# Bias rows of the four gates on SP's queue, and the general expert path as a loop over single experts

## The chip, the core and the metric

The kernel runs on one core of a Trainium2 chip. The metric is the device time of one execution in microseconds. The core has five engines that each work through a queue of their own, strictly in order: TensorE (PE in the profile, with its weight loads as PEld), VectorE (DVE), ScalarE (ACT), GpSimd (POOL) and SyncE (SP), which computes nothing and only issues transfers here. Transfers (DMAs) can be issued from SP, ACT and POOL.

## What is computed

A decoder trunk of two layers on 256 tokens of width 1024, all in float32. Layer 0 mixes tokens with a state-space scan (S5), layer 1 with forgetting attention (FoX) over a shared K and V. After each mixer comes a mixture of experts: 32 experts in four groups, two experts per token. Every sub-layer has a shift, a scale and a gate that depend on a conditioning vector `c`:

```python
def adaln(c, w, b, n):
    mod = jax.nn.silu(c) @ w + b
    return jnp.split(mod, n, axis=-1)

for l in range(DEPTH):
    shift, scale, gate = adaln(c, ada_w[l, 0], ada_b[l, 0], 3)
    ...
    h = h + gate[:, None, :] * mix
    shift, scale, gate = adaln(c, ada_w[l, 1], ada_b[l, 1], 3)
    ...
    h = h + gate[:, None, :] * hier_moe(...)
```

The four gates (`gate`, twice per layer) are what one part of the change touches: `b` is the bias row. The other part touches the sum over the experts:

```python
for e in range(N_EXPERTS):
    y = (jax.nn.silu(t @ w1[e]) * (t @ w3[e])) @ w2[e]
    out = out + gates[:, e:e + 1] * y
```

## The kernel before

**Weights.** All large weights stream once through a ring of slots of 1 MB (`new_slot`, `fetch`, line 67), every transfer issued by SP. `block` takes the next block, `prefetch` asks for one ahead of its use. A transfer waits in SP's queue until its slot is free. In the built program the transfers of SP and ACT also share eight completion counters that they take in turn, so that a transfer waits until the one eight places before it has landed. Which instruction follows which on an engine is settled when the program is built: a planner walks through a simulated timeline and, apart from parts with an order written out by hand (`tc.manual_schedule`), puts what is ready earliest first.

**Gates.** `ada_gate_pe` (lines 175 to 195) makes one gate: GpSimd clears a tile `rows` (line 179, it waits until the tile's last user, often `as_columns` at lines 139 to 141, is done), ACT issues two transfers of 2 KB that put the two halves of the bias into partitions 0 and 32 (line 181), TensorE multiplies four weight blocks (line 184), VectorE adds product and `rows` (line 188), and two matmuls (line 194) and ScalarE (line 195) spread the result over the partitions. It runs four times: in the S5 part (`gb00`, from the list `side`), at the start of the first mixture (`gb01`), in the FoX part (`gb10`) and at the start of the second mixture (`gb11`).

**S5 part.** Before its loop (lines 987 to 1014) stand `drive_u(0)` to `drive_u(2)` (TensorE, line 808), `prepare_b(0)` (VectorE lines 843 to 853, then ScalarE line 855, which copies from the tile `braw`), `flip_b(0)` (TensorE line 864, ScalarE line 867), and `direct(0)` (line 897). In the loop, `drive` (TensorE line 916, VectorE line 921) and the scans (line 935) follow.

**Experts.** In `moe`, each expert has 32 places for tokens (`CAP`). `experts` works through eight sets of four experts: `first` (line 506) and `second` (line 521) are the matmuls with the blocks `wa` and `wb`, `gather` and `scatter` move the tokens. Ahead of the seventh set stands `overflow` (lines 533 to 592): where some expert has more than 32 tokens (`mosti`, read into every engine), a loop over all experts adds what didn't fit; otherwise every engine branches over it (line 535). The inputs of this case don't take it.

Of the kernel before, what the change touches and what calls it, by code (L numbers as in the profile page):

```python
# [10 lines left out]
F32 = mybir.dt.float32  # L11
# [3 lines left out]
AF = mybir.ActivationFunctionType  # L15
OP = mybir.AluOpType
# [6 lines left out]
NE = 32  # L23
CAP = 32
NQ = NE // 4
# [13 lines left out]
def trunk(ctx: ExitStack, tc: tile.TileContext, A, out, ring=12, ring2=4, ring3=5, ring4=3, ring5=4, lpb=2, TK=2):  # L39
    nc = tc.nc  # L40
    V, S, G, PE = nc.vector, nc.scalar, nc.gpsimd, nc.tensor
# [9 lines left out]
    def acc_tile():  # L51
        return psum.tile([128, 512], F32, tag="acc", name="acc", bufs=4)

    def mm_tile():
        return psum.tile([128, 512], F32, tag="mm", name="mm", bufs=4)
# [14 lines left out]
    def block(name, *idx):  # L70
        for i, (b, t) in enumerate(ahead):
            if b == (name, idx):
                del ahead[i]
                return t
        if (name, idx) in later:
            later.remove((name, idx))
        return fetch(A[name][idx])
# [24 lines left out]
    ident = const.tile([128, 128], F32, name="ident")  # L102
# [18 lines left out]
    def sc32(k):  # L121

        return sc[:, k:k + 1].to_broadcast([128, 32])
# [4 lines left out]
    for q in range(4):  # L128
        r = slice(32 * q, 32 * q + 32)
# [45 lines left out]
    def ada_gate_pe(name, j, li, gbc, at_once=False):  # L175

        ps = mm_tile() if at_once else acc_tile()
        rows = small.tile([128, 512], F32, tag="rows", name="rows", bufs=1)
        G.memset(rows, 0.0)
        for n in range(2):  # L180
            nc.scalar.dma_start(rows[32 * n:32 * n + 1, :], A["gbias"][li, n:n + 1, :])
        for b, w in enumerate([block(name, j, b) for b in range(4)]):
            for q in range(4):
                PE.matmul(ps[32 * q:32 * q + 32, :], sc32(2 * b + q // 2), w[:, 512 * q:512 * q + 512],
                          start=b == 0, stop=b == 3)
            if not at_once:
                yield
        ins = V.tensor_tensor(rows, ps, rows, op=OP.add)
        if not at_once:
            tc.keep_in_program_order(ins)  # L190
        yield
        for n in range(2):
            pt = mm_tile()
            PE.matmul(pt, pick[:, n:n + 1].to_broadcast([128, 128]), rows, start=True, stop=True)
            S.activation(gbc[:, 512 * n:512 * n + 512], pt, AF.Copy)
# [136 lines left out]
    def moe(l, sh, g, gbc, c36, slots_):  # L332
# [12 lines left out]
        mb = []  # L345
# [21 lines left out]
        def t2(n, w):  # L367
            return ma.tile([128, 2, w], F32, name=n)
# [78 lines left out]
        scs, xgs, Ps, acc = {}, {}, {}, []  # L447
# [43 lines left out]
        def turned(a):  # L491
            pa = mm_tile()
            for f in range(2):
                PE.transpose(pa[:, 128 * f:128 * f + 128], a[:, 128 * f:128 * f + 128], ident)
            aT = mb[0].tile([128, 256], F32, tag="aT", name="aT", bufs=2)
            V.tensor_copy(aT, pa[:, 0:256])
            return aT
# [35 lines left out]
        def overflow(rv):  # L533

            with tc.If(rv > CAP):
                gov = t2("gov", NE)
                V.tensor_scalar(gov, rk, float(CAP) + 0.5, None, op0=OP.is_gt)
                V.tensor_tensor(gov, gov, gates, op=OP.mult)
                hnT = [mb[0].tile([128, KD, 128], F32, tag="y", name="hnT", bufs=2) for _ in range(2)]
                for i in range(2):  # L540
                    x = mb[0].tile([128, 256], F32, tag="aT", name="dr", bufs=2)[:, 0:128]
                    V.tensor_scalar(x, ident, rstd[:, i:i + 1], None, op0=OP.mult)
                    for kk in range(2):
                        pt = mm_tile()
                        for k4 in range(4):
                            k = 4 * kk + k4
                            o = pt[:, 128 * k4:128 * k4 + 128]
                            PE.matmul(o, h[:, i, 128 * k:128 * k + 128], x, start=True, stop=True)
                            V.tensor_scalar(hnT[i][:, k, :], o, g[:, k:k + 1], sh[:, k:k + 1],
                                            op0=OP.mult, op1=OP.add)  # L550
                with tc.For_i(0, NQ, 1) as q:
                    gcol = t2("gcol", 4)
                    G.dma_start(gcol, gov.rearrange("p i (q s) -> p i q s", s=4)[:, :, bass.ds(q, 1), :]
                                      .rearrange("p i o s -> p i (o s)"))
                    for s in range(4):
                        c = slice(512 * s, 512 * s + 512)

                        def part(name, j):
                            w = mb[0].tile([128, 2, 512], F32, tag="ow", name="ow", bufs=1)
                            G.dma_start(w, A[name][l, bass.ds(q, 1), 2 * j:2 * j + 2, :, c]  # L560
                                              .rearrange("o k p n -> p (o k) n"))
                            return w

                        ph = [mm_tile() for _ in range(2)]
                        for kp in range(4):
                            w = part("wa", kp)
                            for i in range(2):
                                for kk in range(2):
                                    PE.matmul(ph[i], hnT[i][:, 2 * kp + kk, :], w[:, kk],
                                              start=kp + kk == 0, stop=kp == 3 and kk == 1)  # L570
                        aTs = []
                        for i in range(2):
                            a = mb[0].tile([128, 256], F32, tag="a", name="oa", bufs=2)
                            S.activation(a, ph[i][:, 0:256], AF.Silu)
                            V.scalar_tensor_tensor(a, a, gcol[:, i, s:s + 1], ph[i][:, 256:512],
                                                   op0=OP.mult, op1=OP.mult)
                            aTs.append(turned(a))
                        for n in range(2):
                            w = part("wb", n)
                            py = [mm_tile() for _ in range(2)]  # L580
                            for f in range(2):
                                for i in range(2):
                                    PE.matmul(py[i], aTs[i][:, 128 * f:128 * f + 128], w[:, f],
                                              start=f == 0, stop=f == 1)
                            for i in range(2):
                                for c2 in range(2):
                                    r = slice(256 * c2, 256 * c2 + 256)
                                    t = mb[0].tile([128, 256], F32, tag="aT", name="ot", bufs=2)
                                    V.tensor_tensor(t, py[i][:, r], gbc[:, 512 * n + 256 * c2:512 * n + 256 * c2 + 256],
                                                    op=OP.mult)  # L590
                                    PE.matmul(acc[i][n][:, r], ident, t, start=False, stop=False,
                                              skip_group_check=True)

        def start(gated, ssq, fill, after):

# [78 lines left out]
    hnT = sp.tile([128, KD, T], F32, name="hnT")  # L674
# [28 lines left out]
    p, two = exp_parts(sp, ldt, t32)  # L703
# [13 lines left out]
    for b in range(2):  # L717
        r = slice(16 * b, 16 * b + 16)
# [6 lines left out]
    p, two = exp_parts(sp, z, t32)  # L725
# [11 lines left out]
    for b in range(4):  # L737
        r = slice(8 * b, 8 * b + 8)
# [73 lines left out]
    for m in range(2):  # L812
# [3 lines left out]

    steps = [1, 1, 1, 0, 1, 0, 1, 0, 0, 0]
    side = [ada_gate_pe("ada00g", 0, 0, gb00, True),
            ada_cols_pe("ada01", 0, as_shift(C_ADAB + 16, sh01)),
            ada_cols_pe("ada01", 1, as_gain(C_ADAB + 16, C_LNG + 8, g01)),  # L820
            ada_cols_pe("kvada", 0, as_shift(C_ADAB + 64, shkv)),
            ada_cols_pe("kvada", 1, as_gain(C_ADAB + 64, C_KVG, gkv))]
    fill = [ada_gate_pe("ada01", 2, 1, gb01)]


# [205 lines left out]
    def split_w(w):  # L1031
        o = gp.tile([128, 2, 512], F32R, tag="ws", name="ws", bufs=3)
        S.activation(o[:, 0], w, AF.Copy)
        V.tensor_tensor(o[:, 1], w, o[:, 0].bitcast(F32), op=OP.subtract)
        return o
# [10 lines left out]
    for n in range(2):  # L1046
        pg = [mm_tile() for _ in range(2)]
        for m in range(8):
            if m % 4 == 0:
                w = block("woutg", n, m // 4)  # L1050
            o = split_w(w[:, 512 * (m % 4):512 * (m % 4) + 512])
            if n == 0 and m < 7:
                split_u(m + 1)
            for i in range(2):
                for u, b in ((uH, 0), (uL, 0), (uH, 1)):
                    PE.matmul(pg[i], u[:, m, 128 * i:128 * i + 128], o[:, b], start=m == 0 and b == 0 and u is uH,
                              stop=m == 7 and b == 1)
# [563 lines left out]
```

## Time and profile before

| | us |
|---|---|
| median of 3 runs (849.17 to 849.5) | 849.39 |
| the profiled execution | 854.14 |
| its span, first to last instruction | 852.5 |
| TensorE busy | 722.5 (85%) |
| VectorE busy | 410.1 (48%) |
| ScalarE busy | 218.3 (26%) |
| GpSimd busy | 58.3 (7%) |
| moved by DMA | 299.32 MB |

The profiled execution is slower than the timed ones, and 1.64 us of it lie outside its span. "busy" of TensorE holds pipelined matmuls and is not its share of peak. A wait is shown as the idle time of an engine, with what ended it; a wait for several things is put down to the one that came last. Queue instructions (issue, semaphore, branch) are marked with a q behind the engine (ACTq) and don't count as busy. The profile gives TensorE's clock as the share that was granted, 1.0 being 2.4 GHz and 0.5 being 1.2 GHz.

### The profile page before, as it was taken

What the parts mean: (1) busy time and instruction counts of PE and PEld (TensorE: products, weight loads), DVE (VectorE), ACT (ScalarE), POOL (GpSimd) and SP (SyncE); (2) the same over time, 40 slices, a digit from 0 to 9 for tenths busy, and PEclk for the clock granted to TensorE, in tenths of its full rate; (3) what the DMA queues carried; (4) which work ended last, traced back from release to release, by engine and by line L of the source; (5) the groups of instructions that cost most, each with busy time, mean ns of one, the idle gap of its engine ahead of it and who ended that gap; (6) DMA issues with size and microseconds to landing.
All of it is one profiled execution on the core that took longest, in us unless ns stands there. A gap on an engine that the chain in (4) does not pass through costs nothing.

```text
span 852.5 us, 13440 instructions
## 1 busy us (share of the span) xinstructions
PE 722.5 (85%) x5382; PEld 401.3 (47%) x5382; DVE 410.1 (48%) x1069; ACT 218.3 (26%) x498; POOL 58.3 (7%) x52
## 2 busy tenths in 40 slices
PE   2777999898899997576799999899998999887766
PEld 0655776575533333131255567788755334331311
DVE  6657799875322322120355569997553223221102
ACT  4323233162300110010232255556522001100100
POOL 2000000000000000000001202870000000000000
PEclk9988999998999999889799999999989999997898
DMA  9996856687999999999999787552679999999996
GB/s 365 416 420 256 328 218 248 264 344 289 419 420 418 421 418 419 420 416 421 420 418 399 282 324 260 196 188 100 241 306 394 419 419 419 418 419 419 418 418 247
DMA packets 41830, 299.32 MB, mean 351 GB/s; under 512 B 4632, under 2 KB 4760, under 8 KB 5664
## 3 DMA queue, kind: packets, MB, share of 16 engines
q1 hardware_dynamic: 41328, 297.13, 86.3%
q10 hardware_dynamic: 432, 1.25, 0.4%
q8 instruction: 45, 0.74, 0.4%
q14 instruction: 25, 0.20, 0.1%
HBM read 297.31 MB, written 1.05 MB: 350 GB/s over the span
## 4 chain that ended last, share of the span: by engine, by line
PE 47%; DMA 31%; DVE 17%; ACT 2%; issue 2%; POOL 0%; SPq 0%; ACTq 0%; DVEq 0%; POOLq 0%
DMA w<-wa 14%; DMA w<-wb 10%; PE mm L506 8%; PE acc L1199 7%; PE mm L470 5%; PE mm L521 4%; PE acc L528 4%; PE acc L1430 3%; DVE m L921 2%; DMA w<-win 2%; DVE m L935 2%; DMA w<-ada00g 2%; PE mm L169 2%; DMA w<-ada 2%; DVE m L954 2%; PE acc L1393 2%
## 5 line engine op out<-in xcount | busy, mean ns | idle before, releaser
L506 PE MATMUL mm<-w,xg 128*32 128x512 f32 x1024 | 140.0, 637 | 33.6 <-DMA w<-wa 22.7
L506 PEld LDWEIGHTS mm<-w,xg 128*32 128x32 f32 x1024 | 29.4, 111 | 118.3 <-issue 69.1
L521 PE MATMUL mm<-w,aT 128*32 128x512 f32 x512 | 68.4, 650 | 12.1 <-DMA w<-wb 6.3
L1199 PE MATMUL acc<-ws,hn 128*128 128x512 f32 x288 | 77.7, 409 | 0.7 <-DVE ws L1129 0.7
L478 ACT ACTIVATE xg<-mm,sh,g 128x128 f32<-128x128 f32 x64 | 29.3, 457 | 187.0 <-PE mm L470 170.9
L1129 DVE TENSOR_TENSOR ws<-w,ws 128x512 fp32r<-128x512 f32 x80 | 60.7, 768 | 32.7 <-ACT ws L1128 32.5
L470 PE MATMUL mm<-Pr,h 128*128 128x128 f32 x512 | 64.9, 280 | 11.0 <-DVE Pr L458 11.0
L470 PEld LDWEIGHTS mm<-Pr,h 128*128 128x128 f32 x512 | 60.5, 193 | 26.4 <-issue 23.2
L528 PE MATMUL acc<-y,Sc 128*128 128x512 f32 x128 | 64.7, 629 | 6.5 <-DVE y L524 5.7
L1128 ACT ACTIVATE ws<-w 128x512 fp32r<-128x512 f32 x80 | 49.7, 629 | 67.9 <-PE acc L1199 49.5
L476 DVE TENSOR_SCALAR xg<-mm,g,sh 128x128 f32<-128x128 f32 x64 | 26.2, 410 | 75.2 <-ACT xg L478 75.2
L1199 PEld LDWEIGHTS acc<-ws,hn 128*128 128x128 f32 x288 | 51.1, 188 | 23.9 <-issue 7.1
L524 DVE TENSOR_TENSOR y<-mm,gbc 128x512 f32<-128x512 f32 x32 | 22.1, 692 | 67.6 <-PE mm L521 67.3
L489 DVE COPY Sc<-mm 128x256 f32<-128x256 f32 x16 | 6.8, 425 | 86.0 <-PE mm L487 86.0
L511 ACT ACTIVATE a<-mm 128x256 f32<-128x256 f32 x16 | 6.1, 383 | 163.7 <-PE mm L506 163.7
L528 PEld LDWEIGHTS acc<-y,Sc 128*128 128x128 f32 x128 | 22.2, 193 | 45.9 <-issue 28.7
L512 DVE TENSOR_TENSOR a<-a,mm 128x256 f32<-128x256 f32 x16 | 6.7, 419 | 76.9 <-ACT a L511 76.9
L521 PEld LDWEIGHTS mm<-w,aT 128*32 128x32 f32 x512 | 14.1, 114 | 53.6 <-issue 35.4
L984 PE MATMUL acc<-w,uT 128*128 128x512 f32 x64 | 31.7, 642 | 5.7 <-ACT uT L973 5.7
L808 PE MATMUL mm<-hnT,w 128*64 128x128 f32 x512 | 33.3, 291 | 2.7 <-ACT hnT L275 2.7
L1393 PE MATMUL acc<-hn,ws 128*128 128x256 f32 x192 | 29.4, 310 | 5.2 <-DVE ws L1129 5.2
L808 PEld LDWEIGHTS mm<-hnT,w 128*64 128x64 f32 x512 | 31.4, 143 | 4.5 <-ACT hnT L275 3.7
(337 smaller groups left out, 1004.2 us busy)
## 6 DMA issues: line engine op xcount, KB each, us to landing
w<-wa SPq DMA_DIRECT2D x128, 1024.0 KB, 19.9
w<-wb SPq DMA_DIRECT2D x64, 1024.0 KB, 19.9
w<-ada SPq DMA_DIRECT2D x36, 1024.0 KB, 8.8
w<-ada00s SPq DMA_DIRECT2D x8, 1024.0 KB, 18.0
w<-kvada SPq DMA_DIRECT2D x8, 1024.0 KB, 9.1
w<-win SPq DMA_DIRECT2D x4, 1024.0 KB, 18.5
w<-ada00g SPq DMA_DIRECT2D x4, 1024.0 KB, 18.9
w<-woutv SPq DMA_DIRECT2D x4, 1024.0 KB, 17.4
```

The costliest lines, as they stand in the source:

```text
L470: PE.matmul(px[:, 128 * c4:128 * c4 + 128], h[:, i, 128 * c:128 * c + 128], Pr[:, i].rearrange("p a b -> p (a b)"), start=i == 0, stop=i == 1)
L476: V.tensor_scalar(xg[:, c], src, g[:, c:c + 1], sh[:, c:c + 1], op0=OP.mult, op1=OP.add)
L478: S.activation(xg[:, c], src, AF.Identity, bias=sh[:, c:c + 1], scale=g[:, c:c + 1])
L506: PE.matmul(ph[32 * s:32 * s + 32, :], xg[:, k, 32 * s:32 * s + 32], w[:, 512 * s:512 * s + 512], start=k == 0, stop=k == KD - 1)
L521: PE.matmul(py[32 * s:32 * s + 32, :], aT[:, 128 * f + 32 * s:128 * f + 32 * s + 32], w[:, 512 * s:512 * s + 512], start=f == 0, stop=f == 1)
L528: PE.matmul(acc[i][n], scs[q][:, 128 * i:128 * i + 128], y[:, 512 * n:512 * n + 512], start=q == 0, stop=q == NQ - 1, skip_group_check=True)
L808: PE.matmul(ps[64 * v:64 * v + 64, 128 * hh:128 * hh + 128], w[:, k, c0:c0 + 64], hnT[:, k, v::2], start=k == 0 and hh == 0, stop=k == KD ...
L984: PE.matmul(val[t][n], uT[:, m, 128 * t:128 * t + 128], wval[m // 2][:, c0:c0 + 512], start=m == 0, stop=m == 7)
L1128: S.activation(o[:, 0], w, AF.Copy)
L1129: V.tensor_tensor(o[:, 1], w, o[:, 0].bitcast(F32), op=OP.subtract)
L1199: PE.matmul(pk[i], src[:, k, a, 128 * i:128 * i + 128], w[:, b], start=k + a + b == 0, stop=k == KD - 1 and b == 1)
L1393: PE.matmul(po[:, 256 * m2:256 * m2 + 256], w[:, bb, kk, 128 * m2:128 * m2 + 128], hq[:, k, a, :], start=k + a + bb + m2 == 0, stop=k == K ...
```

## The change

In `ada_gate_pe` the two bias transfers are issued by SP in place of ACT. In `overflow` the loop over eight sets with four experts written out in each becomes two nested loops, over the sets and over the four experts of one; the gates of the current expert are kept in column 0 of `gov`, which is shifted by one column per round (two copies) in place of a transfer; the six weight transfers of a round are issued by SP, where 25 were issued by POOL. The products' tile takes another tag, and the scratch space for POOL's transfers is halved. Nothing else is different.

```diff
-            nc.scalar.dma_start(rows[32 * n:32 * n + 1, :], A["gbias"][li, n:n + 1, :])
+            nc.sync.dma_start(rows[32 * n:32 * n + 1, :], A["gbias"][li, n:n + 1, :])
...
-                with tc.For_i(0, NQ, 1) as q:
-                    gcol = t2("gcol", 4)
-                    G.dma_start(gcol, gov.rearrange("p i (q s) -> p i q s", s=4)[:, :, bass.ds(q, 1), :]
-                                      .rearrange("p i o s -> p i (o s)"))
-                    for s in range(4):
-                        c = slice(512 * s, 512 * s + 512)
-
-                        def part(name, j):
-                            w = mb[0].tile([128, 2, 512], F32, tag="ow", name="ow", bufs=1)
-                            G.dma_start(w, A[name][l, bass.ds(q, 1), 2 * j:2 * j + 2, :, c]
-                                              .rearrange("o k p n -> p (o k) n"))
-                            return w
...
+                gnext = t2("gnext", NE)
+                with tc.For_i(0, NQ, 1) as q, tc.For_i(0, 2048, 512) as c:
+
+                    def part(name, j):
+                        w = mb[0].tile([128, 2, 512], F32, tag="ow", name="ow", bufs=1)
+                        nc.sync.dma_start(w, A[name][l, bass.ds(q, 1), 2 * j:2 * j + 2, :, bass.ds(c, 512)]
+                                          .rearrange("o k p n -> p (o k) n"))
+                        return w
...
+                    V.tensor_copy(gnext[:, :, 0:NE - 1], gov[:, :, 1:NE])
+                    V.tensor_copy(gov[:, :, 0:NE - 1], gnext[:, :, 0:NE - 1])
...
-    nc = bacc.Bacc("TRN2", target_bir_lowering=False, num_devices=1, dynamic_dma_scratch_size=2048)
+    nc = bacc.Bacc("TRN2", target_bir_lowering=False, num_devices=1, dynamic_dma_scratch_size=1024)
```

## Rows read from the trace of the kernel before

**Rows 1.** Busy time by stretch: us, then PE, PEld, DVE, ACT, POOL, PEclk, DMA share, GB/s

```profile
44.00:49.40 5.40, 0.00 (x0) 0.00 (x0) 0.54 (x2) 0.34 (x2) 0.00 (x0) 0.98 1.01 417
49.40:57.00 7.60, 7.39 (x58) 6.24 (x60) 2.10 (x7) 2.64 (x8) 0.00 (x0) 0.56 1.01 420
...
90.00:165.00 75.00, 74.05 (x1075) 52.97 (x1074) 73.07 (x160) 23.02 (x67) 0.00 (x0) 1.00 0.73 288
165.00:204.00 39.00, 33.91 (x220) 26.43 (x220) 25.29 (x45) 19.43 (x40) 0.00 (x0) 0.98 0.67 257
...
424.00:600.00 176.00, 165.70 (x925) 118.10 (x924) 130.19 (x281) 85.87 (x179) 49.51 (x27) 0.97 0.71 268
...
732.00:841.00 109.00, 81.78 (x508) 27.32 (x500) 18.39 (x49) 7.02 (x16) 0.00 (x0) 0.88 1.01 417
```

**Rows 2.** Waits between 30 and 58 us: total, times, longest

```profile
ACT ab L855 <- DMA w<-ada00g: 16.6, 1, 16.6
```

**Rows 3.** ScalarE's timeline: start, length, instruction, [idle before <- what ended it]

```profile
30.54 1.93 ACT L275 ACTIVATE hnT<-acc,sh,g 128x256 f32<-128x256 f32 x4 [4.27 <-DVE g L155]
46.35 0.49 ACTq L181 DMA_DIRECT2D rows<-gbias  x1
48.78 0.23 ACTq L181 DMA_DIRECT2D rows<-gbias  x1
49.06 0.51 ACT L855 ACTIVATE ab<-braw 128x128 f32<-128x128 f32 x2 [16.59 <-DMA w<-ada00g]
```

**Rows 4.** SP's timeline, 27 to 63 us: the transfers around the bias rows

```profile
27.39 0.33 SPq L67 DMA_DIRECT2D w<-ada00g  x1
...
43.82 0.33 SPq L67 DMA_DIRECT2D w<-woutv  x1
51.32 11.16 SPq L67 DMA_DIRECT2D w<-ada  x4
```

**Rows 5.** The chain that ended last: start, length, the piece before flip_b(0)

```profile
29.87 18.89 DMA w<-ada00g
```

**Rows 6.** VectorE's timeline, 34 to 57 us

```profile
34.81 0.42 DVE L843 TENSOR_TENSOR abt<-braw,are 128x256 f32<-128x256 f32 x1 [1.76 <-DMA braw<-s5b]
...
56.58 0.69 DVE L921 TENSOR_TENSOR m<-mm,cosT 128x512 f32<-128x512 f32 x1 [4.17 <-PE mm L916]
```

**Rows 7.** TensorE's timeline, 31 to 60 us, and one row at 89.6 us

```profile
31.16 12.70 PE L808 MATMUL mm<-hnT,w 128*64 128x128 f32 x192 [2.75 <-ACT hnT L275]
49.42 1.12 PE L864 MATMUL mm<-ident,ab 128*128 128x128 f32 x4 [5.56 <-ACT ab L855]
...
51.32 2.08 PE L916 MATMUL mm<-uT,bz 128*128 128x128 f32 x8 [0.18 <-ACT bz L867]
53.32 2.40 PE L808 MATMUL mm<-hnT,w 128*64 128x128 f32 x20
55.65 1.34 PE L916 MATMUL mm<-uT,bz 128*128 128x128 f32 x8
...
59.58 0.65 PE L864 MATMUL mm<-ident,ab 128*128 128x128 f32 x4
...
89.60 2.05 PE L916 MATMUL mm<-uT,bz 128*128 128x128 f32 x16
```

**Rows 8.** Line 188: count, shortest/median/longest ns, first to last start

```profile
L188 DVE TENSOR_TENSOR rows<-mm,rows x2: 683/684/684, 76.1 to 505.9; 128x512 f32<-128x512 f32 x2
```

**Rows 9.** Line 535, the branch over the general path: as Rows 8

```profile
L535 POOLq INC_SWDGE_SEM  x2: 142/158/173, 213.6 to 640.3; - x2
L535 PEldq COMPARE_BRANCH  x2: 6157/6164/6172, 358.3 to 785.4; - x2
L535 SPq COMPARE_BRANCH  x2: 50/52/53, 389.0 to 811.7; - x2
```

**Rows 10.** Who waited for line 535, and line 67's transfers from issue to landing

```profile
  PE mm L506: 10.7, 2
...
DMA to landing us min/median/max: 4.8/19.5/21.3
```

More of the change, by code (lines that the diff above doesn't have):

```diff
@@ L550, in overflow @@
                                             op0=OP.mult, op1=OP.add)
-                with tc.For_i(0, NQ, 1) as q:
-                    gcol = t2("gcol", 4)
-                    G.dma_start(gcol, gov.rearrange("p i (q s) -> p i q s", s=4)[:, :, bass.ds(q, 1), :]
-                                      .rearrange("p i o s -> p i (o s)"))
-                    for s in range(4):
-                        c = slice(512 * s, 512 * s + 512)
-                        def part(name, j):
-                            w = mb[0].tile([128, 2, 512], F32, tag="ow", name="ow", bufs=1)
-                            G.dma_start(w, A[name][l, bass.ds(q, 1), 2 * j:2 * j + 2, :, c]
-                                              .rearrange("o k p n -> p (o k) n"))
-                            return w
-                        ph = [mm_tile() for _ in range(2)]
-                        for kp in range(4):
-                            w = part("wa", kp)
+                gnext = t2("gnext", NE)
@@ new lines, in overflow @@
+                with tc.For_i(0, NQ, 1) as q, tc.For_i(0, 2048, 512) as c:
[4 more added lines that the diff above has]
+                        return w
+                    ph = [mm_tile() for _ in range(2)]
+                    for kp in range(4):
+                        w = part("wa", kp)
+                        for i in range(2):
+                            for kk in range(2):
+                                PE.matmul(ph[i], hnT[i][:, 2 * kp + kk, :], w[:, kk],
+                                          start=kp + kk == 0, stop=kp == 3 and kk == 1)
+                    aTs = []
+                    for i in range(2):
+                        a = mb[0].tile([128, 256], F32, tag="a", name="oa", bufs=2)
+                        S.activation(a, ph[i][:, 0:256], AF.Silu)
+                        V.scalar_tensor_tensor(a, a, gov[:, i, 0:1], ph[i][:, 256:512], op0=OP.mult, op1=OP.mult)
+                        aTs.append(turned(a))
+                    V.tensor_copy(gnext[:, :, 0:NE - 1], gov[:, :, 1:NE])
+                    V.tensor_copy(gov[:, :, 0:NE - 1], gnext[:, :, 0:NE - 1])
+                    for n in range(2):
+                        w = part("wb", n)
+                        py = [mm_tile() for _ in range(2)]
+                        for f in range(2):
@@ L567, in overflow @@
                             for i in range(2):
[L568 to L571, printed above, removed]
+                                PE.matmul(py[i], aTs[i][:, 128 * f:128 * f + 128], w[:, f],
+                                          start=f == 0, stop=f == 1)
                         for i in range(2):
[L573 to L592, printed above, removed]
+                            for c2 in range(2):
+                                r = slice(256 * c2, 256 * c2 + 256)
+                                t = mb[0].tile([128, 256], F32, tag="a", name="ot", bufs=2)
+                                V.tensor_tensor(t, py[i][:, r], gbc[:, 512 * n + 256 * c2:512 * n + 256 * c2 + 256],
+                                                op=OP.mult)
+                                PE.matmul(acc[i][n][:, r], ident, t, start=False, stop=False, skip_group_check=True)
```

## The prediction, made before the result was known

> **What bounds the kernel now.** I read the stretches first, because an average over stages with different limits says nothing about one of them. The reader is to see two kinds of stage [rows 1]. In the mixtures (732 to 841 us stands for both) the DMA share is 1.01 at 417 GB/s: there the transfers set the pace, and an engine that gets faster gains nothing. In S5 (90 to 165) VectorE and TensorE are busy for 73.07 and 74.05 of 75 us with the DMA at 0.73, and between 165 and 204 and in FoX (424 to 600) the DMA has room as well (0.67 and 0.71). A shift of work before 204 us therefore moves the moment at which the mixture's stream of weights begins, and with it everything behind.
>
> Second the list of waits at the start of S5, third the timelines of the engines there. ScalarE stands idle for 16.6 us [rows 2] ahead of line 855, and the profile names a weight transfer as releaser that line 855 doesn't read. The timeline tells why [rows 3]: after 32.47 us nothing runs until ACT issues its first bias row at 46.35 and its second at 48.78, and only then comes line 855. ACT works in order, so the waiting transfers held it. What they waited for: SP's third block of `ada00g` was issued at 27.39 [rows 4] and its fourth at 29.87, and the fourth took 18.89 us to land [rows 5]; 27.39 + 18.89 = 46.28 and 29.87 + 18.89 = 48.76, the two issue times of the bias rows. So each row took its turn behind the transfer eight places before it. SP shows the same beat: `woutv` at 43.82, then two beats of about 2.5 us without SP, then `ada` at 51.32 [rows 4]; the two free places are the bias rows'.
>
> Nothing else held line 855: its input `braw` was there at 34.81 us, when VectorE began to read it [rows 6]. TensorE ran out of work at 31.16 + 12.70 = 43.86 and stood for 5.56 us until line 855 let it go on at 49.42 [rows 7].
>
> **The change part by part.** The sum is made against the profiled execution (span 852.5, in all 854.14 us) and then set against the median of 849.39; the difference of 4.75 us between these two is taken to stay as it is.
>
> (a) *The first gate's two transfers leave ACT.* Line 855 can run at 35 us instead of 49, beside line 808, and line 864 starts when TensorE comes free: 5.56 us earlier. VectorE's drive and scans hang on the same matmuls [rows 6], so they follow. Next late are TensorE's own matmuls, then VectorE.
>
> (b) *TensorE's clock.* The stop also costs clock: after 44.00 to 49.40 without a matmul the granted clock is 0.56 from 49.4 to 57 [rows 1], near the lower level of 1.2 GHz; after 12.70 us of unbroken matmuls it would stay high. At full clock, by rows of the same form [rows 7]: line 864 0.65 instead of 1.12, line 916 x8 half of 2.05, so 1.03, instead of 2.08 and again of 1.34, line 808 x20 12.70 / 192 x 20 = 1.32 instead of 2.40. Saved: 0.47 + 1.05 + 1.08 + 0.31 = 2.91. VectorE waits for exactly these until 56.58 [rows 6]. Bounds: 0, if the clock falls in some other short stop, and 2.9. I take 2.2, nearer to the upper end, since ScalarE's two conversions at line 867 stand between lines 864 and 916 and won't shrink. Together with (a): 7.8, bounds 5.6 and 8.5.
>
> (c) *The first gate's rows on SP.* SP takes the same two places in turn (46.35 and 48.78), where now ACT waits and SP has nothing to issue; behind them is queued `ada` at 51.32, which waited anyway. What lies ahead of them in SP's queue: if a row needs as long as a block, 18.89 us, the last lands at 67.7. The reader of the rows is line 188 at 76.1 [rows 8], after the shift of 7.8 at 68.3. Cover: 0.6 us; if it is gone, VectorE waits at line 188 with the scans behind it, microsecond for microsecond. Cost taken: 0.
>
> (d) *The other three gates.* ACT loses six issues of 0.23 to 0.49 us each [rows 3], 1.4 to 2.9 us, none in a stretch that ScalarE bounds: busy 85.87 of 176 us in FoX and 7.02 of 109 in a mixture [rows 1]. On SP they may stand in front of weights until GpSimd has cleared `rows`; eight blocks are under way in the mixtures, and in FoX the DMA has 29% of its time free. 0, between -0.5 and +1.
>
> The Trainium skill ("DMA: Bandwidth & Descriptors", section "Issuing engines are not separate DMA queues") says that issuing from another engine saves only the issue time, which is usually small. By that rule alone (a) and (b) would be nothing and the sum eight issues on an idle engine. Rows 3 speak against it for this place: what ACT loses is not the 0.49 and 0.23 us of issue but the wait in front of them.
>
> (e) *The shorter general path.* It is branched over in both mixtures. TensorE's branch took 6157 and 6172 ns, SP's some 52 ns [rows 9], and TensorE's matmuls waited 10.7 us for the two [rows 10]. With about a quarter of TensorE's instructions in the path both may vanish. I cost that at 0: both lie in stretches of full DMA share [rows 1], and transfers under way take 19.5 us each from issue to landing [rows 10], so the weights go on arriving through a stop of 6. If that cover weren't there, it would be worth up to -10.7.
>
> The Trainium skill ("Runtime: NRT & Kernel Launch", section "Instruction fetch mechanics") has a taken branch stall where its target isn't among the instructions already loaded. TensorE's long branch agrees with that, and the short ones of the engines with less code too.
>
> (f) *The bookkeeping of the skipped path.* An engine that skips transfers has to set their completion counters as if they had run, and in the built program waits first until those counters are at rest; POOL does this now (line 535, 0.14 to 0.17 us, with nothing of its own under way) [rows 9]. After the change SP must do it for six transfers, at its branches at 389.0 and 811.7, with eight blocks under way and behind it all further weights. Lower bound 0: if the six are the next in turn, they are the six oldest, the two youngest still run while SP comes back. Upper bound: if SP waits for all eight, the DMA stands for the start of a fresh transfer, the shortest landing 4.8 [rows 10] less the beat of about 2.5 [rows 4], 2.3 each, 4.6 for two. I take 0.4, near the lower end, because six out of eight, taken in turn, leave two.
>
> Sum: -5.6 - 2.2 + 0 + 0 + 0 + 0.4 = -7.4. Span 845.1, profiled 846.7, median 842.0. The shift is given back nowhere that I can find: what SP fetches after 77 us waits for slots that the shifted matmuls free, and the mixtures' stream starts earlier by the same amount.
>
> **The rivals.**
>
> *It gets slower: the rows come late.* The planner may put the two rows behind the four blocks `ada` (51.32 + 11.16 - 0.33 = 62.15 [rows 4]), and they then land at 62.15 + 18.89 = 81.0, past today's 76.1; line 188 stops VectorE, and the time is 849.4 + 4.9 = 854.3. The point from which it decides: issued after 49.4 they eat the gain, after 76.1 - 18.9 = 57.2 they make the kernel slower than before. For it: a gap of only 0.6 us in (c). Against it: the places of the rows today are ahead of those four blocks. 10%.
>
> *SP drains.* The upper end of (f): 849.4 - 7.8 + 4.6 = 846.2, with the smaller gain 848.4. For it: all weights stand behind SP's wait. 10%.
>
> *No difference.* The skill's rule above, or ACT is held at this place by something else: 849.4. For it, that the releaser in the list of waits is a weight block, which still lands when it did; against it, that line 855 needs `braw` alone. 6%.
>
> *The branches count too.* -7.4 - 10.7: 831.3. Against it the full DMA share. 4%.
>
> **How the numbers follow.** The forecast has 70%: 842.0, between 849.4 - 8.5 - 0.9 = 840.0 and 849.4 - 5.6 + 1.2 = 845. With the drained SP up to 848.4 this holds 80%, so the range is 840.0 to 848.4. A measurement of this kernel can tell about 0.2% (1.7 us) from no change. Faster: forecast, branches and most of the drained SP, 0.82; same: no difference and the rest, 0.08; slower: 0.10.
>
> **What would show it.** Right: line 855 at about 35 us, line 864 with no wait at about 44, a clock near 1.0 from 44 to 50, VectorE's first line 921 at 48 to 51, line 188 at about 68 without a wait, every stage behind shifted by 6 to 8 us, DMA share 1.01 in both mixtures, TensorE's branches short without any gain there. Wrong: line 864 still waiting for ScalarE; line 188 waiting for the bias rows; a slice of lower DMA share after SP's branches; a mixture that begins earlier and doesn't end earlier.

## The result, and the profile after

The changed kernel takes 842.51 us (median of 4 runs, 841.31 to 844.87) where the kernel before, on the same chip, takes 849.44 (4 runs): a ratio of 0.992, 95% interval 0.990 to 0.994, 6.9 us less. The prediction said 842.0. The profiled execution took 844.87 us, with a span of 843.1, against 854.14 and 852.5. Behind the shortened part of `overflow` the line numbers of the changed kernel are 3 lower: line 852 is line 855 of before, 861 is 864, 805 is 808, 913 is 916 and 918 is 921.

First ScalarE's timeline, 28 to 60 us (start, length, instruction, and in brackets the idle time before it and what ended it). It answers to rows 2 and 3:

```profile
30.32 1.93 ACT L275 ACTIVATE hnT<-acc,sh,g 128x256 f32<-128x256 f32 x4 [4.41 <-DVE g L155]
34.58 0.51 ACT L852 ACTIVATE ab<-braw 128x128 f32<-128x128 f32 x2 [2.33 <-DMA braw<-s5b]
```

The 16.59 us of idle time are 2.33, and what ended them is the transfer that the line reads. TensorE's timeline, 28 to 50 us, answers to rows 7:

```profile
30.94 13.65 PE L805 MATMUL mm<-hnT,w 128*64 128x128 f32 x192 [2.75 <-ACT hnT L275]
44.52 0.66 PE L861 MATMUL mm<-ident,ab 128*128 128x128 f32 x4
...
45.96 1.16 PE L913 MATMUL mm<-uT,bz 128*128 128x128 f32 x8 [0.38 <-ACT bz L864]
47.04 1.37 PE L805 MATMUL mm<-hnT,w 128*64 128x128 f32 x20
48.34 1.16 PE L913 MATMUL mm<-uT,bz 128*128 128x128 f32 x8
```

Line 861 has no bracket: TensorE goes from line 805 into it without a stop. And the same forms take less time, most of them little more than half: 0.66 where line 864 took 1.12, 1.16 and 1.16 where line 916 took 2.08 and 1.34, 1.37 where line 808 x20 took 2.40. TensorE, VectorE and ScalarE run the same instructions in the same order in both kernels, so no other order is behind this. The busy times by stretch say why; their columns are those of rows 1, and the third row is the mixture of rows 1, moved by 9.5 us with the kernel:

```profile
44.00:49.40 5.40, 5.02 (x68) 4.17 (x62) 1.91 (x7) 2.04 (x5) 0.00 (x0) 1.00 1.00 413
49.40:57.00 7.60, 7.60 (x87) 4.59 (x87) 7.46 (x17) 2.04 (x5) 0.00 (x0) 1.00 1.02 419
...
722.50:831.50 109.00, 80.37 (x508) 27.20 (x500) 18.19 (x49) 7.02 (x16) 0.00 (x0) 0.91 1.01 417
```

The granted clock from 44 to 57 is 1.00, the level of 2.4 GHz, where before it was 0.56 from 49.4 on, and the mixture still runs at a DMA share of 1.01. VectorE's timeline, 44 to 58 us, has its first row of the drive 7.49 us earlier than 56.58 [rows 6]:

```profile
49.09 0.69 DVE L918 TENSOR_TENSOR m<-mm,cosT 128x512 f32<-128x512 f32 x1 [2.16 <-PE mm L913]
```

SP's timeline, 43 to 63 us, shows the two bias rows in the turns that ACT had [rows 4], ahead of the four blocks `ada`:

```profile
43.27 0.33 SPq L67 DMA_DIRECT2D w<-woutv  x1
45.93 2.67 SPq L181 DMA_DIRECT2D rows<-gbias  x2
50.92 7.98 SPq L67 DMA_DIRECT2D w<-ada  x4
```

Line 188, the reader of the rows (count, shortest/median/longest ns, first to last start), answers to rows 8; it waits for nothing in any of its four places. The first line is of before, and completes rows 8:

```profile
L188 DVE TENSOR_TENSOR rows<-acc,rows x2: 683/684/685, 224.5 to 651.6; 128x512 f32<-128x512 f32 x2
```

```profile
L188 DVE TENSOR_TENSOR rows<-mm,rows x2: 684/684/684, 68.6 to 499.1; 128x512 f32<-128x512 f32 x2
L188 DVE TENSOR_TENSOR rows<-acc,rows x2: 683/683/683, 217.8 to 641.9; 128x512 f32<-128x512 f32 x2
```

Its four starts, the gates `gb00`, `gb01`, `gb10` and `gb11`, make marks through the kernel. Before they stood at 76.1, 224.5, 505.9 and 651.6, and the span ended at 852.5; the shifts are 7.5, 6.7, 6.9, 9.7 and 9.4 us. So the gain is made ahead of 68 us, and until 499 it stays within 0.8 us of that. The step from 6.9 to 9.7 lies in FoX, and it goes with the clock (last section).

The branch over the general path, as in rows 9, and the two places where SP does the bookkeeping, in SP's timeline:

```profile
L535 SPq EVENT_SEMAPHORE  x12: 17/17/17, 384.0 to 817.1; - x12
L535 PEldq COMPARE_BRANCH  x2: 318/335/352, 351.0 to 776.5; - x2
L535 SPq COMPARE_BRANCH  x2: 45/49/53, 382.0 to 801.4; - x2
```

```profile
381.60 16.32 SPq L67 DMA_DIRECT2D w<-wb  x4
...
801.01 16.59 SPq L67 DMA_DIRECT2D w<-wa  x2
817.70 2.01 SPq L67 DMA_DIRECT2D w<-wb  x4
```

TensorE's two branches, 6157 and 6172 ns before, take 318 and 352. SP now stands from its branch at 801.4 until its last wait of line 535 at 817.1, nearly 16 us in which it issues no weights, and then makes up for it: four issues in 2.01 us. The DMA hardly notices (busy by stretch, columns as in rows 1):

```profile
813.00:816.00 3.00, 1.07 (x8) 0.16 (x8) 0.00 (x0) 0.00 (x0) 0.00 (x0) 1.00 1.00 415
816.00:819.00 3.00, 1.07 (x8) 0.16 (x8) 0.00 (x0) 0.00 (x0) 0.00 (x0) 1.00 0.96 385
```

A share of 0.96 for 3 us is 0.1 us of transfers.

### The profile page after: what moved, and what is told of

The parts are those of the page before. It is cut to its first block, busy times and chain, and to the rows that moved or that the text cites. A ratio compares the mean times of both kernels' runs of the same rounds, so it can differ in the third digit from the quotient of the medians.

```text
span 843.1 us, 13421 instructions
## 1 busy us (share of the span) xinstructions
PE 719.4 (85%) x5382; PEld 397.4 (47%) x5382; DVE 410.0 (49%) x1069; ACT 218.4 (26%) x498; POOL 57.8 (7%) x52
## 5 line engine op out<-in xcount | busy, mean ns | idle before, releaser
L521 PE MATMUL mm<-w,aT 128*32 128x512 f32 x512 | 70.5, 665 | 14.6 <-DMA w<-wb 9.0
L528 PEld LDWEIGHTS acc<-y,Sc 128*128 128x128 f32 x128 | 23.0, 200 | 48.1 <-issue 30.9
```

The lines of the kernel that those rows point to most:

```text
L521: PE.matmul(py[32 * s:32 * s + 32, :], aT[:, 128 * f + 32 * s:128 * f + 32 * s + 32], w[:, 512 * s:512 * s + 512], start=f == 0, stop=f == 1)
L528: PE.matmul(acc[i][n], scs[q][:, 128 * i:128 * i + 128], y[:, 512 * n:512 * n + 512], start=q == 0, stop=q == NQ - 1, skip_group_check=True)
```

## The experiments

The kernel before ran beside each group, on the same chip: 850.79 us (32 runs) beside e1 to e4, 851.43 (19) beside e6 to e9, 849.08 (17) beside e10 to e13. Every ratio is against the one beside it, with its 95% interval.

### Which part of the change carries the gain: e1 to e4

**e1, only the bias rows**, with the general path of before:

```diff
-            nc.scalar.dma_start(rows[32 * n:32 * n + 1, :], A["gbias"][li, n:n + 1, :])
+            nc.sync.dma_start(rows[32 * n:32 * n + 1, :], A["gbias"][li, n:n + 1, :])
```

> The kernel before with the bias rows on SP's queue and the general path as it was, so that TensorE's long branch (two times 6.2 us) stays. If the gain comes from the rows alone, the time is that of the changed kernel, 842 to 843 against 849.4, and TensorE still stands for about 5 us behind each branch. If the shorter branch of the changed kernel carries part of it (10.7 us of TensorE's time went there), this kernel stays 2 to 5 us above the changed one, 844 to 848.

Measured: 844.73 us (12 runs), ratio 0.993 (0.990 to 0.995). TensorE's long branches are still there, and its matmuls wait for them as before (line 535, as in rows 9 and 10):

```profile
L535 PEldq COMPARE_BRANCH  x2: 6212/6234/6257, 350.2 to 774.2; - x2
...
  PE mm L506: 10.8, 2
```

So the rows alone bring 6.1 us with the long branches in place: most of the gain, though not clearly the whole of it. The changed kernel, measured three times, came out at 6.9, 9.7 (e7) and 8.0 us (e11) under the kernel before.

**e2, only the loop**: the changed kernel with its rows back on ACT. It holds all that belongs to the new general path, the transfers on SP and the scratch space among it.

> The kernel before with the new general path alone, the bias rows stay on ACT. If the branch is hidden behind the stream of weights, and SP's wait for its six oldest transfers costs nothing, the time is that of before, 849.4 within 0.7, although TensorE's branch falls from 6.2 to 0.3 us. If the branch counts, up to 10.7 less, 839 to 846; if SP's wait drains the transfers, 1 to 5 more, 850.4 to 854.

Measured: 848.64 (12 runs), ratio 0.998 (0.995 to 1.000); the branches are as short as in the changed kernel. That left 0 to -4 us open, so it ran again with e10 to e12:

> e2 once more (the new general path, all bias rows on ACT), where 0 to -4 us stood open. Theory, that TensorE's branch is hidden by full DMA share: within 0.2% of the kernel before, ratio 0.998 to 1.002. Rival, that the shorter branches are worth a part of their 10.7 us: ratio 0.993 to 0.997.

Measured: 846.72 (12 runs), ratio 0.998 (0.996 to 1.000). That is -2.2 and -2.4 us, where 10.7 had gone into TensorE's waits for the branches [rows 10]. Neither interval alone excludes nothing at all; weighted together they give -1.7 us, from -3.1 to -0.3, so a small gain of the loop is likely. The profiles lean the same way at the first branch only: from `gb01` to `gb10` the five kernels with the long branches (before, e1, e3, e4, e9) took 281.4 to 283.2 us, the eight with the short ones, without the draining e6, 277.2 to 281.3; from `gb11` to the end it is 200.0 to 201.0 and 199.0 to 201.6. These are single executions with different clocks, and which part of the loop brings the gain wasn't tried.

**e3, only the first gate's rows**, and **e4, only the other three**, both with the general path of before:

```diff
+            (nc.sync if li == 0 else nc.scalar).dma_start(rows[32 * n:32 * n + 1, :], A["gbias"][li, n:n + 1, :])
...
+            (nc.scalar if li == 0 else nc.sync).dma_start(rows[32 * n:32 * n + 1, :], A["gbias"][li, n:n + 1, :])
```

> The kernel before with the rows of the first gate alone on SP. If the wait ahead of line 855 in S5 is the whole of it, the time is 842 to 843, as with all four. If the other three gates carry a part (in the profiles FoX is some 2 us shorter after the change), 844 to 847.

> The kernel before with the rows of the other three gates on SP, the first stays on ACT. If only the first gate matters: 849.4 within 0.7. If the others carry a part: 847 to 848.5; if a row that stands in SP's queue behind GpSimd's clearing holds up weights: above 850.

Measured: e3 844.51 (9 runs), ratio 0.993 (0.990 to 0.995); e4 848.45 (12 runs), ratio 0.997 (0.995 to 1.000). The medians of e3 and e1 differ by 0.2 us: by these the two transfers of the first gate are the whole gain of the rows. Alone, the other three come out at -2.3 us, at the edge of what can be told; on top of the first gate (e1 against e3) they add nothing.

### Is it SP's queue, or only that ACT is free: e9

The kernel before, with the first gate's rows on GpSimd; the order of TensorE, VectorE and ScalarE is that of e3, instruction by instruction.

```diff
+            (G if li == 0 else nc.scalar).dma_start(rows[32 * n:32 * n + 1, :], A["gbias"][li, n:n + 1, :])
```

> The kernel before with one edit: the first gate's two bias transfers are issued by GpSimd; the other three gates stay on ACT and the general path is the old one. The order of TensorE, VectorE and ScalarE is that of e3 row by row. Theory, that the gain comes from ACT no longer standing ahead of line 855, whoever takes the transfers: ratio 0.990 to 0.995 against the kernel before, as e3 (0.9925), line 864 without a wait at about 44.5, line 188 at 67 to 69. Rival, that SP's queue matters as such (the turns that the rows take there): ratio nearer to 1.0. Second rival, that a transfer of GpSimd's comes late behind the clearing of the tile: line 188 waits after 68 and the gain is smaller by as much.

Measured: 845.06 (8 runs), ratio 0.992 (0.989 to 0.995), as e3. GpSimd's, TensorE's and SP's timelines, 25 to 60 us:

```profile
30.45 1.21 POOL L181 DMA_DIRECT2D rows<-gbias  x2 [0.31 <-POOL rows L179]
```

```profile
43.62 0.66 PE L864 MATMUL mm<-ident,ab 128*128 128x128 f32 x4
```

```profile
43.78 0.33 SPq L67 DMA_DIRECT2D w<-woutv  x1
46.27 7.83 SPq L67 DMA_DIRECT2D w<-ada  x4
```

GpSimd issues both rows from 30.45 on, right behind the clearing of the tile and without any turn, and SP's `ada` comes at 46.27, one beat behind `woutv`: the two free beats of rows 4 are gone. That shows whose they were. And the gain is the same on a third queue, so it comes from what the rows no longer stand in front of. The Trainium skill ("DMA: Bandwidth & Descriptors", section "Issuing engines are not separate DMA queues") counts the issue time alone as what another engine can save. Here the runs don't agree: two issues of 0.49 and 0.23 us [rows 3] were worth some 6 us, because ACT waited in front of them with work behind.

### What a full drain costs: e6

The changed kernel, with each `wb` transfer of the skipped loop issued in two halves. The skipped path then holds eight transfers, and SP has to wait for all eight counters. The order of TensorE is unchanged.

```diff
-                        w = part("wb", n)
+                        w = mb[0].tile([128, 2, 512], F32, tag="ow", name="ow", bufs=1)
+                        for kk in range(2):
+                            nc.sync.dma_start(w[:, kk:kk + 1], A["wb"][l, bass.ds(q, 1), 2 * n + kk:2 * n + kk + 1, :,
+                                                                       bass.ds(c, 512)]
+                                              .rearrange("o k p n -> p (o k) n"))
```

> The changed kernel with the two wb transfers of a round of the general path issued in halves, so that the skipped path holds eight transfers in place of six and SP has to wait for all eight completion counters at its two branches. Theory of the prediction's upper bound: the DMA stands for the start of a fresh transfer, 2.3 us each, the kernel 3 to 5 us slower than the changed kernel beside it, and a slice behind each branch with a DMA share clearly under 1.0. Rival, that even a full drain is taken up by the blocks that TensorE has in stock: within 1.5 us of it.

The changed kernel ran beside it as the mark:

> The changed kernel once more, as the mark for e6 and e8 on the same chip: ratio 0.990 to 0.995 against the kernel before.

Measured: e6 848.18 (12 runs), ratio 0.996 (0.993 to 0.998); e7 841.76 (6 runs), ratio 0.989 (0.985 to 0.992), a little below what was expected of it. e6 is 6.4 us slower than the changed kernel beside it. Busy by stretch behind SP's second branch, and SP's timeline:

```profile
819.00:822.00 3.00, 2.00 (x12) 0.27 (x16) 0.00 (x0) 0.00 (x0) 0.00 (x0) 0.50 0.85 352
822.00:825.00 3.00, 2.46 (x12) 0.33 (x16) 0.00 (x0) 0.00 (x0) 0.00 (x0) 0.50 0.08 33
825.00:828.00 3.00, 1.05 (x8) 0.00 (x0) 0.00 (x0) 0.00 (x0) 0.00 (x0) 0.90 0.81 268
```

```profile
803.10 21.75 SPq L67 DMA_DIRECT2D w<-wa  x2
824.96 2.01 SPq L67 DMA_DIRECT2D w<-wb  x4
```

SP issues its next block at the end of the first row, at 824.5, when hardly anything is under way any more (a share of 0.08 from 822 to 825). Missing are (0.15 + 0.92 + 0.19) x 3 = 3.8 us of transfers; behind the first branch it is 4.0 in the same way. So two transfers more in the path decide between 0.1 us of lost transfers and a kernel that is 6.4 us slower, and the prediction's bound for a drain, 2.3 us each, was too low: 0.5 of the 3.8 us are the tail in which the last transfers end, and the pause with the new start takes 3.3.

### What is late next: e8, e10, e12

After the change TensorE's 192 matmuls of line 805 stand ahead of line 861. e8 plans `flip_b(0)` and `direct(0)` ahead of the third `drive_u`:

```diff
     prepare_b(0)
-    prepare_c(0)
-    drive_u(2, mm_tile())
     flip_b(0)
+    prepare_c(0)
     pk = mm_tile()
     direct(0, pk[:, 0:64])
     direct_d(0, pk[:, 0:64])
+    drive_u(2, mm_tile())
```

> The changed kernel with flip_b(0) and direct(0) planned ahead of prepare_c(0) and drive_u(2), so that line 861 stands behind 64 matmuls of line 805 and not behind 96 or more. Theory, that after the change line 805 ahead of line 861 is what is late next in this stretch: VectorE's first line 918 comes 3 to 4.5 us earlier and the time falls by as much, to a ratio of 0.985 to 0.990 against the kernel before. Rival, that VectorE's own work ahead of line 918 or the last third of line 805 is needed just as soon: within 1 us of the changed kernel.

Measured: 834.05 (6 runs), ratio 0.980 (0.976 to 0.983), 7.7 us less than e7 beside it. But VectorE's first line 918 came at 47.04, 2 us earlier and not 3 to 4.5, and the planner had also ordered parts of the first mixture and of FoX anew. e10 takes the two apart: it is e8 with `drive_u(2)` behind `drive(0)` in the loop instead, and with that TensorE's order behind this stretch, the mixtures and FoX among it, is the changed kernel's.

```diff
-    drive_u(2, mm_tile())
...
         if i < 8:
             drive(i)
+        if i == 0:
+            drive_u(2, mm_tile())
```

> The changed kernel with flip_b(0) and direct(0) ahead of prepare_c(0), and drive_u(2) behind drive(0). Against the changed kernel TensorE's order differs only in this stretch (line 861 behind 64 matmuls of line 805 as planned, not 96), and the order of all that follows, the mixtures and FoX among it, is the same; in e8 the planner had also ordered parts of the first mixture and of FoX anew. Theory, that TensorE's line 805 ahead of line 861 is what is late next: VectorE's first line 918 comes at about 46, 3 us ahead of the changed kernel's 49.1, the stretches behind it shift by as much, and the time is 2 to 4 us under the changed kernel beside it. Rival 1, that e8's gain of 7.7 us came from the first stretch as a whole: 6 us or more under it. Rival 2, that e8's gain came from the other order of the later stretches: within 1.5 us of the changed kernel. A wait at line 188 for the bias rows (it would now come at about 65.5) would show how long the rows take.

> The changed kernel once more, as the mark for e10, e12 and e13 on the same chip: ratio 0.988 to 0.994 against the kernel before.

> e8 once more. If its gain is real, it is 4 us or more under the changed kernel beside it, and if that was spread between runs, within 4 us of it.

Measured: e10 839.07 (6 runs), ratio 0.988 (0.985 to 0.991); e11, the changed kernel, 841.04 (6 runs), ratio 0.991 (0.988 to 0.994); e12, that is e8 again, 832.37 (6 runs), ratio 0.980 (0.977 to 0.984). TensorE's and VectorE's timelines of e10, 30 to 50 us:

```profile
30.93 9.08 PE L805 MATMUL mm<-hnT,w 128*64 128x128 f32 x128 [2.75 <-ACT hnT L275]
39.95 0.66 PE L861 MATMUL mm<-ident,ab 128*128 128x128 f32 x4
```

```profile
45.63 0.69 DVE L918 TENSOR_TENSOR m<-mm,cosT 128x512 f32<-128x512 f32 x1
```

Line 861 now comes at 39.95, and line 918 at 45.63 without a bracket: VectorE's own work ends there. From the profiles, worked out from the starts of line 918 and of line 188:

| | first 918 | to gb01 | gb01 to gb10 | gb10 to gb11 (FoX) | gb11 to end |
|---|---|---|---|---|---|
| changed kernel | 49.1 | 168.7 | 281.3 | 142.8 | 201.2 |
| e7, the same | 48.1 | 168.0 | 277.3 | 142.9 | 200.5 |
| e11, the same | 49.0 | 168.8 | 278.5 | 143.6 | 199.4 |
| e10 | 45.6 | 168.6 | 277.2 | 142.9 | 200.7 |
| e8 | 47.0 | 167.9 | 279.5 | 140.8 | 199.9 |
| e12, the same | 46.1 | 166.8 | 278.2 | 139.2 | 201.6 |

e10's 2.5 to 3.5 us at the start, against the three executions of the changed kernel, are 1.9 to 3.6 at the second gate (214.2 against 216.1 to 217.8). In the time it is 2.0 us under the changed kernel, at the edge of the 2 to 4 expected, and the intervals of the two overlap, so a gain of e10 alone isn't shown. e8's gain came twice, 7.7 and 8.7 us. The profiles, three of the changed kernel and two of e8, show 1 to 3 us of it at the start, 0 to 2 in the rest of the S5 part and 2 to 4 in FoX, where the order is another. That this order makes FoX shorter wasn't tried by itself. e8 is the fastest of all versions here, some 17 us under the kernel before.

## Why the prediction was right, point by point

**(a) ACT no longer stands ahead of line 855.** Right in mechanism (e1, e3, e9), and a little too large for this execution: line 861 came 4.90 us earlier and not 5.56. The term missed that line 805 isn't always 12.70 us: it took 13.65 here, 0.95 longer, having begun 0.22 earlier, and line 861 begins 0.07 ahead of its modelled end. Busy by stretch in the first half of line 805, of before and then of after, columns as in rows 1:

```profile
31.16:37.50 6.34, 6.34 (x84) 6.34 (x86) 3.91 (x10) 1.31 (x3) 0.00 (x0) 0.73 1.02 418
```

```profile
30.94:37.50 6.56, 6.56 (x74) 6.56 (x75) 4.06 (x11) 1.82 (x5) 0.00 (x0) 0.61 1.02 414
```

The granted clock was at its upper level for less of this half (0.61 against 0.73, third column from the right). Two more executions of the changed kernel, e7 and e11, show 12.37 and 13.64 us for the same matmuls.

**(b) The clock.** Right, and for the two executions compared here taken too low: of the 7.49 us by which line 918 moved, 4.90 are the start, so 2.59 came from the clock, where 2.2 stood in the sum and 2.91 was the bound. That 7.49 is so near to 7.8 is partly luck, as the two errors nearly cancel. Other profiles confirm both terms and show their spread. In the four kernels with the first gate's rows on ACT (before, e2, e4, e13) TensorE stood for 4.5 to 5.8 us, line 861 (864 where the long path is) began at 49.1 to 49.4, and from there to the first line 918 (or 921) it took 5.84 to 7.20 us. In the seven without, and with the same order (the changed kernel, e1, e3, e6, e7, e9, e11), line 861 began at 43.4 to 45.2 without a stop, and to line 918 it took 4.55 to 4.57 us. So the clock was worth 1.3 to 2.6 us, by the execution. TensorE's timelines of e4 and then of e2 show the two ends, the same x20 at 1.36 and at 2.40:

```profile
49.41 1.05 PE L864 MATMUL mm<-ident,ab 128*128 128x128 f32 x4 [4.79 <-ACT ab L855]
...
53.21 1.36 PE L808 MATMUL mm<-hnT,w 128*64 128x128 f32 x20
```

```profile
49.09 0.74 PE L861 MATMUL mm<-ident,ab 128*128 128x128 f32 x4 [4.54 <-ACT ab L852]
...
52.69 2.40 PE L805 MATMUL mm<-hnT,w 128*64 128x128 f32 x20
```

**(c) The first gate's rows on SP.** Right: issued at 45.93 and 48.37, and no wait at line 188 at 68.6. The rival of the late rows needed 49.4. How long a row takes on SP's queue isn't shown; in e3 line 188 began at 67.46 without a wait, 18.7 us behind SP's second row (48.73), so it is at most that. On GpSimd's queue in e9 the two rows landed 6.3 and 6.4 us after their issue, a third of the 18.89 us that the prediction had as its longest case.

**(d) The other three gates.** Taken at 0, with -0.5 to +1 as bounds. e1 against e3 agrees, e4 (-2.3, interval -4.2 to -0.2) would make the lower bound too narrow. What this is worth stays open between 0 and e4's -2.3 us.

**(e) TensorE's branches.** Right that they would vanish and be worth little; at 0 the term was probably too small, since e2 and e13 give the loop some 2 of the 10.7 us. That the cover is the one named fits the DMA share of 1.01 before and after; no run took the cover away. That the long branch belongs to the long path is shown too: with some 25 transfers and four experts written out it is 6.2 us in e1, with one expert in the loop 0.33. The Trainium skill ("Runtime: NRT & Kernel Launch", section "Instruction fetch mechanics") has a branch stall where its target isn't loaded, and these two durations fit that; what was loaded no run here shows.

**(f) SP's bookkeeping.** Right that two transfers of eight are cover enough: 0.1 us of transfers lost at a branch where 0.2 was taken. The upper bound was mis-sized: e6 shows 3.8 and 4.0 us of lost transfers per drain for the 2.3 of the prediction, and 6.4 us in the time for its 4.6.

**The rivals.** Late rows and draining SP are refuted by the rows above, "no difference" by the result, and that the branches count with their full 10.7 us by e2 and e13, which leave at most 4. The shift was given back nowhere beyond 0.8 us: the marks move by 6.7 to 7.5 us until 499.

**The number.** That 842.51 is so near to 842.0 is luck in part. In the time the rows alone brought 6.1 to 6.4 us (e1, e3, e9), where (a) to (d) summed to 7.8, and the loop some 2 us, where (e) and (f) together cost 0.4; the two differences go against each other. The first lies within the intervals of these runs; the second lies just outside those of e2 and e13, whose upper ends are 0.1 and 0.3 us. The sum's own bounds also give 840.4 and 845.2 for the forecast, from -0.5 of (d) with 0 of (f) and from +1 with 0.4, and not the 840.0 and 845 that it states; nothing hangs on that.

## What to carry to other kernels

A transfer on a computing engine's queue can cost what the engine waits in front of it (16.6 us of ACT here), and not its issue alone (0.49 and 0.23 us): look for a wait whose releaser the waiting line doesn't read. Work out from the timeline which transfer's landing it waited for, and what stands behind it in order. And before transfers go into a path that is branched over, count them against those that may be under way: in this kernel six of eight cost 0.1 us of transfers at a branch, eight of eight 6.4 us of time.

## What the runs showed that I had not expected

One program doesn't take one time: the median of the kernel before was 849.08 to 851.43 us on the chips used, and its 68 runs beside the experiments reach from 847.3 to 855.2. They go with TensorE's mean granted clock: the 12 runs with a clock under 0.936 have a median of 854.1 us, the 19 from 0.936 to 0.942 851.3, the 30 up to 0.948 849.8, and the 7 from 0.948 on 848.6. Where such a step is made can be read in FoX. TensorE's timelines of two executions of the changed kernel, the one of the result first, then e11:

```profile
601.28 1.18 PE L1427 MATMUL acc<-ws,oT 128*128 128x512 f32 x4 [1.29 <-ACT oT L1418]
602.30 1.04 PE L1339 MATMUL mm<-ident,pr 128*128 128x128 f32 x8
603.09 3.50 PE L1427 MATMUL acc<-ws,oT 128*128 128x512 f32 x14
```

```profile
598.50 1.20 PE L1427 MATMUL acc<-ws,oT 128*128 128x512 f32 x4 [1.30 <-ACT oT L1418]
599.53 1.87 PE L1339 MATMUL mm<-ident,pr 128*128 128x128 f32 x8
601.06 4.38 PE L1427 MATMUL acc<-ws,oT 128*128 128x512 f32 x14
```

The stop ahead of them is the same, 1.29 and 1.30 us. Then the second and third rows, the same matmuls, take 1.04 + 3.50 = 4.54 us in the one and 6.25 in the other. Busy by stretch, the same matmuls in each, has the granted clock in the third column from the right:

```profile
601.28:606.53 5.25, 5.25 (x27) 4.06 (x27) 3.38 (x5) 2.29 (x4) 0.00 (x0) 1.00 1.00 418
```

```profile
598.50:605.37 6.87, 6.87 (x27) 5.48 (x27) 3.38 (x5) 2.29 (x4) 0.00 (x0) 0.75 0.77 320
```

1.00 is the upper level throughout, 0.75 a part of the stretch at the lower. With one order of instructions FoX (from `gb10` to `gb11`) took 142.8, 142.9 and 143.6 us in three executions of the changed kernel. That is also the step from 6.9 to 9.7 us between the profiles of before and after: FoX 145.7 in the one and 142.8 in the other. Whether the change has a hand in it stays open. Of the five kernels with the long path, whose TensorE, VectorE and ScalarE all have one order, the three with the last gates' rows on ACT (before, e3, e9) took 145.7 each and the two with them on SP (e1, e4) 141.3 each; with the loop it is 144.0 and 142.8 on ACT (e2, e13) and 142.8 to 143.6 on SP. Against it stands that the medians of e1 and e3 differ by only 0.2 us.

What decides in which execution the clock falls, the runs don't show. But a stop that the engine takes at every run is a risk of a microsecond or two of clock besides its own length, and (b) was one of these: behind the stops of 4.5 to 5.8 us it cost between 1.3 and 2.6 us in the four profiles.
